# Row variances of a 67 MB array: large loads halved by partitions over two queues, and the columns of a group shared out anew

## The chip, the core and the metric

The kernel runs on one core of a Trainium2 chip. Its engines work side by side: TensorE (not used here), VectorE (DVE), ScalarE (ACT), GpSimd (POOL) and SyncE (SP), which here only issues transfers. ACT can issue transfers too, from its own instruction stream. Data move between HBM and the on-chip memory (SBUF, 128 partitions) by DMA. The metric is the device time of one execution in microseconds (us); lower is better.

## The reference

```python
batch, seq, dim = 32, 512, 1024
x = np.random.randn(batch, seq, dim).astype(np.float32)

mean_sq = np.mean(x**2, axis=-1)
sq_mean = np.mean(x, axis=-1)**2
return (mean_sq - sq_mean).astype(np.float32)
```

For each of the 32 x 512 = 16384 rows of 1024 numbers the output is the mean of the squares minus the square of the mean, which is the variance of the row. 67.1 MB are read and 64 KB are written.

## The kernel before

**Layout.** The 16384 rows are spread over the 128 partitions, 128 rows to each. A row in each of the 128 partitions together is called a column: the kernel has `ncols` = 128 columns of 128 x 1024 numbers, and the result is a tile `mv` whose plane 1 holds one number per partition and column. Rows that lie next to each other in HBM go to the same partition, so n columns of one partition are one piece of n x 4 KB in HBM.

**Stages.** Columns 0 to 103 come in 13 groups of 8 (`GROUP`, `NGROUPS`). A group is one load of 4 MB (`load`, line 45, issued by SP) into a tile `xt` of the pool `xpool`, which has three buffers. So three loads are issued at once, and the load of group g+3 waits until every reader of group g is done. The last 24 columns are the end: loads of 6, 6, 4, 3, 2 and 1 columns, and then two columns in halves of 512 numbers, all into one tile `xt_end` of its own, whose loads wait for no reader.

**Who computes a column.** There are two ways.

- DVE (`dve_halves`, line 111): two `bn_stats` on 512 numbers each, which leave counts, means and sums of squared deviations. In the groups and in the first two end loads these pieces are collected in a tile of statistics and are joined for many columns at once by ten small POOL instructions (`join`, lines 90 to 102). In the later end loads DVE joins them itself with `bn_aggr` (lines 169 and 179).
- ACT (`act_cols`): a `Copy` with a sum over the row, scaled to the negative mean (line 121), and then a `Square` with this mean as its bias and a sum over the row (line 129), which is the variance.

In even groups ACT takes 3 of 8 columns and DVE 5, in odd groups 2 and 6 (`ACT_OF_GROUP`). `END_WHO` names the engine of each end column: 8 go to ACT and 14 to DVE, and the two halved columns go to DVE as well.

**Order.** A scheduler turns this program into one instruction order for each engine and queue and puts in the semaphore waits. In the kernel before, the order on each engine is the order of the program text: 13 group loads, then the ten end loads, then the store of columns 16 to 127 on SP (line 52). The store of columns 0 to 15 stands on ACT between the groups and the end columns. Each engine works through its list strictly in order: an instruction that waits holds everything behind it.

Of the kernel before, what the change touches and what calls it, by code (L numbers as in the profile page):

```python
# [11 lines left out]
def kernel(  # L12
# [8 lines left out]
    nc = tc.nc  # L21
    P = nc.NUM_PARTITIONS
    FP32 = mybir.dt.float32
    ACTF = mybir.ActivationFunctionType
    ALU = mybir.AluOpType

    xf = x.flatten_outer_dims()
    N, D = xf.shape
# [8 lines left out]
    def block_of(c):  # L37
        return next(b for b in BLOCKS if b[0] <= c < b[0] + b[1])

    def load(dst, c0, n, f0=0, f=D):  # L40

        b0, pitch, row0 = block_of(c0)
        assert c0 + n <= b0 + pitch
        ap = [[pitch * D, P], [D, n], [1, f]] if n > 1 else [[pitch * D, P], [1, f]]
        nc.sync.dma_start(  # L45
            out=dst,
            in_=dataclasses.replace(xf, offset=(row0 + c0 - b0) * D + f0, ap=ap),
        )

    def store(engine, block):  # L50
# [6 lines left out]
    GROUP = 8  # L57
    NGROUPS = 13
    END0 = GROUP * NGROUPS
    ACT_OF_GROUP = (3, 2)  # L60

    END_LOADS = [6, 6, 4, 3, 2, 1]
    END_WHO = "AADDDDAADDDDDADDDADADA"
# [2 lines left out]
    xpool = ctx.enter_context(tc.tile_pool(name="xpool", bufs=3))  # L66
    spool = ctx.enter_context(tc.tile_pool(name="spool", bufs=4))
    opool = ctx.enter_context(tc.tile_pool(name="opool", bufs=1))

    mv = opool.tile([P, 2, ncols], FP32)  # L70
    neg_mean = opool.tile([P, ncols], FP32)
    junk = [opool.tile([P, D], mybir.dt.bfloat16, name=f"junk{i}") for i in range(4)]
    xt_end = opool.tile([P, ncols - END0, D], FP32)
    stats_of = {}

    def stats_block(name, groups, each):

        st = opool.tile([P, groups * each, 2, 6], FP32, name=name)
        return st

    def join(st, groups, each, first, step, skip):

        n = groups * each
        part = st.rearrange("p n h (e s) -> p n (h e) s", s=3)
        mean, m2 = part[:, :, :, 1], part[:, :, :, 2]
        two = opool.tile([P, n, 2], FP32, name=f"two{first}")
        mu = opool.tile([P, n, 1], FP32, name=f"mu{first}")
        dev = opool.tile([P, n, 4], FP32, name=f"dev{first}")
        g = nc.gpsimd
        g.tensor_tensor(out=two, in0=mean[:, :, 0:2], in1=mean[:, :, 2:4], op=ALU.add)  # L90
        g.tensor_tensor(out=mu, in0=two[:, :, 0:1], in1=two[:, :, 1:2], op=ALU.add)
        g.tensor_scalar(out=mu, in0=mu, scalar1=0.25, scalar2=None, op0=ALU.mult)  # L92
        g.tensor_tensor(out=dev, in0=mean, in1=mu.to_broadcast([P, n, 4]), op=ALU.subtract)  # L93
        g.tensor_tensor(out=dev, in0=dev, in1=dev, op=ALU.mult)  # L94
        g.tensor_scalar(out=dev, in0=dev, scalar1=D / 4.0, scalar2=None, op0=ALU.mult)  # L95
        g.tensor_tensor(out=dev, in0=dev, in1=m2, op=ALU.add)  # L96
        g.tensor_tensor(out=two, in0=dev[:, :, 0:2], in1=dev[:, :, 2:4], op=ALU.add)  # L97
        g.tensor_tensor(out=mu, in0=two[:, :, 0:1], in1=two[:, :, 1:2], op=ALU.add)
        var = mv[:, 1, first : first + groups * step].rearrange(
            "p (g k) -> p g k", k=step  # L100
        )[:, :, skip : skip + each]
        g.tensor_scalar(  # L102
            out=var,
            in0=mu.rearrange("p (g k) o -> p g (k o)", k=each),
            scalar1=1.0 / D,
            scalar2=None,
            op0=ALU.mult,
        )

    def dve_half(stats, h, xh):  # L110
        nc.vector.bn_stats(out=stats[:, h, :], in_=xh)  # L111

    def dve_halves(stats, xcol):
        dve_half(stats, 0, xcol[:, :H])
        dve_half(stats, 1, xcol[:, H:])

    def act_cols(cols):

        s = D ** -0.5
        for i, (xcol, c) in enumerate(cols):  # L120
            nc.scalar.activation(  # L121
                out=junk[i],
                in_=xcol,
                func=ACTF.Copy,
                scale=-s / D,
                accum_out=neg_mean[:, c : c + 1],
            )
        for i, (xcol, c) in enumerate(cols):
            nc.scalar.activation(  # L129
                out=junk[3],  # L130
                in_=xcol,
                func=ACTF.Square,
                scale=s,
                bias=neg_mean[:, c : c + 1],
                accum_out=mv[:, 1, c : c + 1],
            )

    body = []
    for par in range(2):
        groups = len(range(par, NGROUPS, 2))  # L140
        each = GROUP - ACT_OF_GROUP[par]
        body.append((stats_block(f"stats{par}", groups, each), groups, each))
    for g in range(NGROUPS):
        c0 = g * GROUP
        xt = xpool.tile([P, GROUP, D], FP32, name="xt")
        load(xt, c0, GROUP)
        skip = ACT_OF_GROUP[g % 2]
        act_cols([(xt[:, k, :], c0 + k) for k in range(skip)])
        st, _, each = body[g % 2]
        for k in range(skip, GROUP):  # L150
            dve_halves(st[:, g // 2 * each + k - skip, :, :], xt[:, k, :])
    for par, (st, groups, each) in enumerate(body):
        join(st, groups, each, par * GROUP, 2 * GROUP, ACT_OF_GROUP[par])

    nb, step, skip = BATCH
    each = step - skip
    st_end = stats_block("stats_end", nb, each)
    k = 0
    for b, n in enumerate(END_LOADS):
        load(xt_end[:, k : k + n, :] if n > 1 else xt_end[:, k, :], END0 + k, n)  # L160
        mine = range(k, k + n)
        act_cols([(xt_end[:, j, :], END0 + j) for j in mine if END_WHO[j] == "A"])
        for j in mine:
            if END_WHO[j] == "D" and b < nb:
                dve_halves(st_end[:, b * each + j - k - skip, :, :], xt_end[:, j, :])
            elif END_WHO[j] == "D":
                stats = spool.tile([P, 2, 6], FP32, name="stats")
                dve_halves(stats, xt_end[:, j, :])
                nc.vector.bn_aggr(out=mv[:, :, END0 + j], in_=stats)  # L169
        if b == nb - 1:  # L170
            join(st_end, nb, each, END0, step, skip)
        k += n
    for j in range(k, ncols - END0):
        stats = spool.tile([P, 2, 6], FP32, name="stats")
        for h in range(2):
            xh = xt_end[:, j, h * H : (h + 1) * H]
            load(xh, END0 + j, 1, h * H, H)
            dve_half(stats, h, xh)
        nc.vector.bn_aggr(out=mv[:, :, END0 + j], in_=stats)  # L179
# [33 lines left out]
```

## Time and profile before

| what | value |
|---|---|
| median of 3 runs | 165.49 us (165.44 to 165.92) |
| profiled execution: span from first to last instruction | 163.5 us |
| DVE busy | 106.1 us (65%) |
| ACT busy | 94.9 us (58%) |
| POOL busy | 10.2 us (6%) |
| DMA queue of SP | 67.17 MB, 96.3% of the 16 DMA engines' span |
| mean rate over the span | 411 GB/s |

How to read it: the span runs from the first to the last instruction of one profiled execution. The timed median lies 165.49 - 163.5 = 2.0 us above it, and the prediction carries these 2.0 us along as a constant for what lies around the span. "L121" is line 121 of the kernel. "SPq" and "ACTq" are transfers issued by SP and ACT. In a row of the timeline, the first number is the start and the second the duration, in us; what stands in brackets is how long the engine sat idle and what ended that.

### The profile page before, as it was taken

What the parts mean: (1) busy time and instruction counts of PE and PEld (TensorE: products, weight loads), DVE (VectorE), ACT (ScalarE), POOL (GpSimd) and SP (SyncE); (2) the same over time, 40 slices, a digit from 0 to 9 for tenths busy, and PEclk for the clock granted to TensorE, in tenths of its full rate; (3) what the DMA queues carried; (4) which work ended last, traced back from release to release, by engine and by line L of the source; (5) the groups of instructions that cost most, each with busy time, mean ns of one, the idle gap of its engine ahead of it and who ended that gap; (6) DMA issues with size and microseconds to landing.
All of it is one profiled execution on the core that took longest, in us unless ns stands there. A gap on an engine that the chain in (4) does not pass through costs nothing.

```text
span 163.5 us, 462 instructions
## 1 busy us (share of the span) xinstructions
DVE 106.1 (65%) x182; ACT 94.9 (58%) x165; POOL 10.2 (6%) x34
## 2 busy tenths in 40 slices
DVE  0008559393793917949097682949559396859993
ACT  3008756195733937349390693809755195499892
POOL 0000000000000000000000000000000635302200
DMA  7899898998999999999999999999999999999970
GB/s 257 385 481 417 385 513 385 417 481 385 481 417 385 485 409 393 497 393 425 465 393 473 417 393 505 393 401 489 393 465 425 421 391 475 391 440 409 408 291 14
DMA packets 3602, 67.19 MB, mean 411 GB/s; under 512 B 656, under 2 KB 656, under 8 KB 1296
## 3 DMA queue, kind: packets, MB, share of 16 engines
q1 hardware_dynamic: 3456, 67.17, 96.3%
q10 hardware_dynamic: 144, 0.01, 0.1%
q14 instruction: 2, 0.02, 0.0%
HBM read 67.11 MB, written 0.07 MB: 411 GB/s over the span
## 4 chain that ended last, share of the span: by engine, by line
DMA 79%; DVE 11%; ACT 8%; issue 0%; SPq 0%
DMA xt<-in_x_dram 62%; DMA xt_end<-in_x_dram 17%; DVE stats L111 10%; ACT junk L129 4%; ACT junk L121 4%; DVE mv L179 0%; SPq L45 0%
## 5 line engine op out<-in xcount | busy, mean ns | idle before, releaser
L111 DVE BATCH_NORM_STATS2 stats<-xt 128x6 f32<-128x512 f32 x142 | 85.5, 678 | 50.7 <-DMA xt<-in_x_dram 50.7
L121 ACT ACTIVATE junk<-xt 128x1024 bf16<-128x1024 f32 x33 | 34.5, 1046 | 59.2 <-DMA xt<-in_x_dram 59.2
L129 ACT ACTIVATE junk<-xt,neg_mean 128x1024 bf16<-128x1024 f32 x33 | 37.7, 1142 | 0.6
L111 DVE BATCH_NORM_STATS2 stats_end<-xt_end 128x6 f32<-128x512 f32 x16 | 9.7, 680 | 3.7 <-DMA xt_end<-in_x_dram 3.7
L121 ACT ACTIVATE junk<-xt_end 128x1024 bf16<-128x1024 f32 x8 | 8.4, 1046 | 5.0 <-POOL mv L102 4.2
L111 DVE BATCH_NORM_STATS2 stats<-xt_end 128x6 f32<-128x512 f32 x16 | 10.1, 666 | 0.1
L129 ACT ACTIVATE junk<-xt_end,neg_mean 128x1024 bf16<-128x1024 f32 x8 | 9.2, 1144 | 0.2
L90 POOL TENSOR_TENSOR two<-stats 128x72 f32<-128x72 f32 (+1 forms) x2 | 0.8, 406 | 131.3 <-DVE stats L111 131.3
L129 ACT ACTIVATION_READ_ACCUMULATOR junk<-xt,neg_mean 128x1 f32 x33 | 6.2, 186 | 0.0
L121 ACT ACTIVATION_READ_ACCUMULATOR junk<-xt 128x1 f32 x33 | 6.2, 186 | 0.0
L121 ACT ACT_TABLE_LOAD x1 | 1.3, 1283 | 0.7 <-PEq L197 0.7
L121 ACT ACTIVATION_READ_ACCUMULATOR junk<-xt_end 128x1 f32 x8 | 1.5, 186 | 0.0
L129 ACT ACTIVATION_READ_ACCUMULATOR junk<-xt_end,neg_mean 128x1 f32 x8 | 1.5, 186 | 0.0
L95 POOL TENSOR_SCALAR dev<-dev 128x144 f32<-128x144 f32 (+2 forms) x3 | 1.4, 472 | 0.3
L169 DVE BATCH_NORM_AGGREGATE mv<-stats 128x2 f32<-128x12 f32 x6 | 1.2, 203 | 0.1
L94 POOL TENSOR_TENSOR dev<-dev 128x144 f32<-128x144 f32 (+2 forms) x3 | 1.1, 362 | 0.2
L96 POOL TENSOR_TENSOR dev<-dev,stats 128x144 f32<-128x144 f32 (+1 forms) x2 | 1.1, 528 | 0.2
L93 POOL TENSOR_TENSOR dev<-stats,mu 128x144 f32<-128x144 f32 (+1 forms) x2 | 0.9, 470 | 0.2
L102 POOL TENSOR_SCALAR mv<-mu 128x36 f32<-128x36 f32 (+2 forms) x3 | 0.9, 287 | 0.3
L92 POOL TENSOR_SCALAR mu<-mu 128x36 f32<-128x36 f32 (+2 forms) x3 | 0.9, 284 | 0.3
L97 POOL TENSOR_TENSOR two<-dev 128x72 f32<-128x72 f32 (+2 forms) x3 | 0.8, 276 | 0.2
L90 POOL TENSOR_TENSOR two<-stats_end 128x16 f32<-128x16 f32 x1 | 0.2, 233 | 8.9 <-DVE stats_end L111 8.9
(9 smaller groups left out, 2.7 us busy)
## 6 DMA issues: line engine op xcount, KB each, us to landing
xt<-in_x_dram SPq DMA_DIRECT2D x13, 4096.0 KB, 22.2
xt_end<-in_x_dram SPq DMA_DIRECT2D x2, 3072.0 KB, 32.2
xt_end<-in_x_dram SPq DMA_DIRECT2D x1, 2048.0 KB, 40.0
xt_end<-in_x_dram SPq DMA_DIRECT2D x1, 1536.0 KB, 43.2
xt_end<-in_x_dram SPq DMA_DIRECT2D x1, 1024.0 KB, 45.1
xt_end<-in_x_dram SPq DMA_DIRECT2D x4, 256.0 KB, 15.3
xt_end<-in_x_dram SPq DMA_DIRECT2D x1, 512.0 KB, 36.7
out_dram<-mv SPq DMA_DIRECT2D x1, 56.0 KB, 1.6
```

Source lines behind the costliest of these rows:

```text
L90: g.tensor_tensor(out=two, in0=mean[:, :, 0:2], in1=mean[:, :, 2:4], op=ALU.add)
L92: g.tensor_scalar(out=mu, in0=mu, scalar1=0.25, scalar2=None, op0=ALU.mult)
L93: g.tensor_tensor(out=dev, in0=mean, in1=mu.to_broadcast([P, n, 4]), op=ALU.subtract)
L94: g.tensor_tensor(out=dev, in0=dev, in1=dev, op=ALU.mult)
L95: g.tensor_scalar(out=dev, in0=dev, scalar1=D / 4.0, scalar2=None, op0=ALU.mult)
L96: g.tensor_tensor(out=dev, in0=dev, in1=m2, op=ALU.add)
L97: g.tensor_tensor(out=two, in0=dev[:, :, 0:2], in1=dev[:, :, 2:4], op=ALU.add)
L102: g.tensor_scalar(out=var, in0=mu.rearrange("p (g k) o -> p g (k o)", k=each), scalar1=1.0 / D, scalar2=None, op0=ALU.mult,)
L111: nc.vector.bn_stats(out=stats[:, h, :], in_=xh)
L121: nc.scalar.activation(out=junk[i], in_=xcol, func=ACTF.Copy, scale=-s / D, accum_out=neg_mean[:, c : c + 1],)
L129: nc.scalar.activation(out=junk[3], in_=xcol, func=ACTF.Square, scale=s, bias=neg_mean[:, c : c + 1], accum_out=mv[:, 1, c : c + 1],)
L169: nc.vector.bn_aggr(out=mv[:, :, END0 + j], in_=stats)
```

## The change

- Each of the 13 group loads becomes two of 2 MB: partitions 0 to 63 from SP's queue and partitions 64 to 127 from ACT's queue (`load_group`). Three groups are loaded ahead of the loop, and the load of group g+3 is written behind the work on group g.
- In each group the columns 0 and 1 are treated in a third way: DVE sums both rows with one `tensor_reduce`, ACT squares each with a sum over the row, and three POOL instructions after the loop turn the two sums into the variance for all groups at once. Column 2 is ACT's in the old way, columns 3 to 7 are DVE's in the old way.
- The collected statistics are split by the first seven and the last six groups, and the first join is written behind group 6.
- The end (`END_LOADS`, `END_WHO`) stays as it is in the text.

```diff
-    def load(dst, c0, n, f0=0, f=D):
+    def load(dst, c0, n, f0=0, f=D, p0=0, p=P, engine=nc.sync):
...
-        ap = [[pitch * D, P], [D, n], [1, f]] if n > 1 else [[pitch * D, P], [1, f]]
-        nc.sync.dma_start(
+        ap = [[pitch * D, p], [D, n], [1, f]] if n > 1 else [[pitch * D, p], [1, f]]
+        engine.dma_start(
             out=dst,
-            in_=dataclasses.replace(xf, offset=(row0 + c0 - b0) * D + f0, ap=ap),
+            in_=dataclasses.replace(
+                xf, offset=(row0 + p0 * pitch + c0 - b0) * D + f0, ap=ap
+            ),
         )
...
-    ACT_OF_GROUP = (3, 2)
+    SUMS = 2
+    SKIP = 3
+    AHEAD = 3
...
+    def load_group(g):
+
+        xt = xpool.tile([P, GROUP, D], FP32, name="xt")
+        c0 = g * GROUP
+        load(xt[: P // 2], c0, GROUP, p0=0, p=P // 2)
+        load(xt[P // 2 :], c0, GROUP, p0=P // 2, p=P // 2, engine=nc.scalar)
+        return xt
+
+    each = GROUP - SKIP
+    halves = (NGROUPS + 1) // 2
...
+    total = opool.tile([P, NGROUPS, SUMS], FP32, name="total")
+    meansq = opool.tile([P, NGROUPS, SUMS], FP32, name="meansq")
+    xts = [load_group(g) for g in range(AHEAD)]
     for g in range(NGROUPS):
         c0 = g * GROUP
-        xt = xpool.tile([P, GROUP, D], FP32, name="xt")
-        load(xt, c0, GROUP)
-        skip = ACT_OF_GROUP[g % 2]
-        act_cols([(xt[:, k, :], c0 + k) for k in range(skip)])
-        st, _, each = body[g % 2]
-        for k in range(skip, GROUP):
-            dve_halves(st[:, g // 2 * each + k - skip, :, :], xt[:, k, :])
-    for par, (st, groups, each) in enumerate(body):
-        join(st, groups, each, par * GROUP, 2 * GROUP, ACT_OF_GROUP[par])
+        xt = xts[g]
+        nc.vector.tensor_reduce(
+            out=total[:, g, :], in_=xt[:, :SUMS, :], axis=mybir.AxisListType.X, op=ALU.add
+        )
+        for k in range(SUMS):
+            nc.scalar.activation(
+                out=junk[k],
+                in_=xt[:, k, :],
+                func=ACTF.Square,
+                scale=D ** -0.5,
+                accum_out=meansq[:, g, k : k + 1],
+            )
+        act_cols([(xt[:, k, :], c0 + k) for k in range(SUMS, SKIP)])
+        st = parts[g // halves][0]
+        for k in range(SKIP, GROUP):
+            dve_halves(st[:, g % halves * each + k - SKIP, :, :], xt[:, k, :])
+        if g + AHEAD < NGROUPS:
+            xts.append(load_group(g + AHEAD))
+        if g == halves - 1:
+            join(parts[0][0], halves, each, 0, GROUP, SKIP)
+    join(parts[1][0], NGROUPS - halves, each, halves * GROUP, GROUP, SKIP)
+    sq = opool.tile([P, NGROUPS, SUMS], FP32, name="sq")
+    nc.gpsimd.tensor_tensor(out=sq, in0=total, in1=total, op=ALU.mult)
+    nc.gpsimd.tensor_scalar(out=sq, in0=sq, scalar1=1.0 / (D * D), scalar2=None, op0=ALU.mult)
+    nc.gpsimd.tensor_tensor(
+        out=mv[:, 1, :END0].rearrange("p (g k) -> p g k", k=GROUP)[:, :, :SUMS],
+        in0=meansq,
+        in1=sq,
+        op=ALU.subtract,
+    )
```

The scheduler orders the changed program differently from its text, and this is part of what runs:

- **SP:** the loads of groups 0, 1, 2 (lower halves), the first end load, group 3, the second end load, groups 4 and 5, the third end load, and so on; the last three are the last end half, group 11 and group 12, and then the store.
- **DVE:** the end columns are worked between the groups, in the order in which their loads stand on SP; the last work is group 12.
- **ACT:** three upper-half loads and the table load, then the groups, with the upper-half load of group g+3 among the work of group g+1. All eight end columns stand behind the wait for group 12. Behind this wait come, in this order: a Square of group 12, the Copy of group 11, an end Copy, the Square of group 11, a Square of group 12, an end Copy, the Copy of group 12, the store of columns 0 to 15, the Square of group 12, five pairs of an end Copy and an end Square, one more end Copy, and three end Squares.

More of the change, by code (lines that the diff above doesn't have):

```diff
@@ L73 @@
     xt_end = opool.tile([P, ncols - END0, D], FP32)
-    stats_of = {}
     def stats_block(name, groups, each):
@@ L136, in act_cols @@
             )
[L138 to L142, printed above, removed]
+    def load_group(g):
[5 more added lines that the diff above has]
+    each = GROUP - SKIP
@@ L143 @@
+    halves = (NGROUPS + 1) // 2
+    parts = [(stats_block("stats0", halves, each), halves), (stats_block("stats1", NGROUPS - halves, each), NGROUPS - halves)]
+    total = opool.tile([P, NGROUPS, SUMS], FP32, name="total")
+    meansq = opool.tile([P, NGROUPS, SUMS], FP32, name="meansq")
+    xts = [load_group(g) for g in range(AHEAD)]
     for g in range(NGROUPS):
         c0 = g * GROUP
-        xt = xpool.tile([P, GROUP, D], FP32, name="xt")
-        load(xt, c0, GROUP)
-        skip = ACT_OF_GROUP[g % 2]
```

## The prediction

> **What bounds the kernel now.** I read the page first (busy shares, then the chain that ended last), then the waits, then the engines and DMA by stretches, and last the timeline of the end. The first line below is from the page's busy times, the second from its chain, the next two from the waits (total, times, longest), the next five from the stretches (length; DVE, ACT and POOL busy with their counts; clock; DMA share; GB/s), and the last three from the page's DMA issues (median from issue to landing).
>
> ```profile
> DVE 106.1 (65%) x182; ACT 94.9 (58%) x165; POOL 10.2 (6%) x34
> ...
> DMA 79%; DVE 11%; ACT 8%; issue 0%; SPq 0%
> ...
> ACT junk L121 <- DMA xt<-in_x_dram: 59.2, 13, 10.7
> DVE stats L111 <- DMA xt<-in_x_dram: 50.7, 13, 12.7
> ...
> 20.00:60.00 40.00, 26.50 (x44) 22.80 (x40) 0.00 (x0) 1.00 1.00 431
> 60.00:100.00 40.00, 26.50 (x44) 22.80 (x40) 0.00 (x0) 1.00 1.00 433
> 100.00:140.00 40.00, 29.02 (x49) 22.81 (x40) 6.95 (x18) 1.00 1.00 430
> 158.00:160.00 2.00, 1.97 (x5) 1.97 (x5) 0.00 (x0) 1.00 0.20 74
> 160.00:163.50 3.50, 0.80 (x3) 0.60 (x2) 0.00 (x0) 1.00 0.06 16
> ...
> xt<-in_x_dram SPq DMA_DIRECT2D x13, 4096.0 KB, 22.2
> out_dram<-mv SPq DMA_DIRECT2D x1, 56.0 KB, 1.6
> out_dram<-mv ACTq DMA_DIRECT2D x1, 8.0 KB, 9.0
> ```
>
> No engine is near its limit, and both wait for a load before every group. From 20 to 140 us the DMA engines are busy all the time (share 1.00) at 430 to 433 GB/s. The kernel is the transfer of 67.1 MB plus a start and an end. The last line of the fence matters below: a store of 8 KB on ACT's queue, issued while SP's queue was full, took 9.0 us, the one of 56 KB with nothing beside it 1.6 us. A second queue beside the first therefore does not pass it, it takes turns with its large pieces.
>
> The timeline gives the pace of the loads and the end (start, duration; in brackets idle time and what ended it):
>
> ```profile
> 22.45 7.22 DVE L111 BATCH_NORM_STATS2 stats<-xt 128x6 f32<-128x512 f32 x12 [3.68 <-DMA xt<-in_x_dram]
> ...
> 130.18 6.03 DVE L111 BATCH_NORM_STATS2 stats<-xt 128x6 f32<-128x512 f32 x10 [2.49 <-DMA xt<-in_x_dram]
> ...
> 155.86 1.06 ACT L121 ACTIVATE junk<-xt_end 128x1024 bf16<-128x1024 f32 x1
> 157.04 1.15 ACT L129 ACTIVATE junk<-xt_end,neg_mean 128x1024 bf16<-128x1024 f32 x1
> 158.19 1.04 ACT L121 ACTIVATE junk<-xt_end 128x1024 bf16<-128x1024 f32 x1
> ...
> 159.36 1.23 DVE L111 BATCH_NORM_STATS2 stats<-xt_end 128x6 f32<-128x512 f32 x2
> 160.63 0.21 DVE L179 BATCH_NORM_AGGREGATE mv<-stats 128x2 f32<-128x12 f32 x1
> 160.98 0.35 SPq L52 DMA_DIRECT2D out_dram<-mv  x1
> ```
>
> Group 1 starts at 22.45, group 12 at 130.18: 107.73 / 11 = 9.79 us for 4 MB. Counted back, the stream starts at 22.45 - 2 x 9.79 = 2.9 us. The last two pieces of statistics start at 159.36, right behind the work before them, so the last load landed at about 159.4 (call it T); the end loads took 159.4 - 130.2 = 29.2 us. From the last result (160.84) to the end of the span are 2.7 us of store. So the time is T plus 1.4 of work, 2.7 of store and the 2.0 us between span and median: 165.5.
>
> **The change, part by part.**
>
> *The end.* In the text the end columns come last; in the built order their loads stand among the group loads on SP, so the last thing to land is group 12, and DVE and ACT have work left then. For DVE: one `tensor_reduce` and ten statistics, which took 6.03 us. The `tensor_reduce` is not in the trace; ten statistics at 603 ns each for 512 numbers bound it above (2048 numbers, 2.41 us), and below the same row less 0.11 us of fixed time (an aggregate starts 0.11 to 0.12 us before what follows it): 2048 x (0.603 - 0.11) / 512 + 0.11 = 2.08 us. I take 2.4. Then comes the join, 4.5 us for 35 columns in the trace (136.29 to 140.83). That is T + 13.
>
> ACT is worse. All its eight end columns stand behind its wait for group 12. After T it still has four Squares of groups at 1.15, four Copies at 1.04, an issue of a store at 0.37, five end pairs (Copy to Square 157.04 - 155.86 = 1.18, Square to Copy 158.19 - 157.04 = 1.15, so 2.33), one Copy at 1.18 and three Squares at 1.25 (two in a row in the chain that ended last: 1.25 each): 4.60 + 4.16 + 0.37 + 11.65 + 1.18 + 3.75 = 25.7 us. The Square without a bias is not in the trace; between 1.04 (Copy) and 1.25 it moves this sum by under 0.5. The store on ACT waits for the POOL instruction that subtracts, which needs the last plain Square (T + 5.6) and some 0.3 us more: done before ACT gets there at T + 7.8. The last store on SP waits for ACT's last Square, so POOL's and DVE's T + 13 is covered by ACT. New: time = T + 25.7 + 2.7 + 2.0 = T + 30.4, where it was T + 6.1. This is 24.3 us whatever the loads do, and as ACT idles before each group it has no backlog at T to add.
>
> *DVE and ACT in the groups.* DVE per group 6.03 + 2.4 = 8.4 us instead of 6.03 or 7.22; in all 13 x 8.4 + 21.4 for the end columns (9.7 + 10.1 + 1.2 + 0.4) = 131 us, below the 159 of loads. ACT has 4.6 instead of 4.5 to 6.9. Both lie beside loads at 9.79 us a group or slower: nothing. POOL's three new instructions and the table load, now behind ACT's three issues (1.28 us, beside the first load): nothing.
>
> *Waits and issues.* 26 issues instead of 13, at 0.33 us: beside loads. ACT's last reader of group g now stands behind its wait for group g+1, so the buffer comes free not 7.2 us after landing, but 9.8 + 2.3 = 12.1 us after it. When the next load is issued, group g+2 still has 7.5 us to go, against 2.2 us from the first issue (0.72) to the start of the stream: nothing, with 5 us to spare. Behind ACT's issue, which waits for DVE as well, stand only ACT's own Copies; after an end load of four DVE columns (4.85 us) this wait is up to 1.2 us longer, inside ACT's idle time. SP's end loads need no reader and fill its queue while it waits.
>
> *The halves.* This decides. No row shows a transfer to fewer than 128 partitions. Low end: time goes by bytes, a half takes 4.9 us, and a group 9.79 as now. A gain below that I exclude at the share of 1.00. High end: time goes by the bytes of a partition, a half takes as long as the whole load, and as the two queues take turns by large pieces (the 9.0 us row), a group takes 19.58 us. The nearest row is the whole load: same 32 KB in each partition, same pieces, only fewer partitions. The 9.0 us row also says that the second queue brings no overlap of its own. I take the high end. The end loads keep their 128 partitions; opposite a half, they cost between nothing and their 29.2 us; I take the middle, 14.6. T = 2.9 + 13 x 19.58 + 14.6 = 272.0, and the time 272.0 + 30.4 = 302.4 us; between the bounds for the end loads 288 to 317.
>
> [...]
>
> **The rivals.**
>
> - *The halves run at full speed together.* For it: the DMA share counts 16 engines, and 64 partitions are still enough pieces for all of them. Against it: the nearest row, and the turns of the two queues. Then T = 159.4 and only the end is paid: 189.8 us.
> - *The halves overlap in part.* If engines get out of step, so that some move lower halves while others move upper ones, a group lies between: 14.7 us in the middle. T = 2.9 + 191.1 + 14.6 = 208.6, time 239.0; with the end loads from nothing to 29.2, 224 to 254. For it: a second queue always offers the other half; against it: each queue also runs alone while the other waits for its buffer.
> - *Not slower.* One queue might be what limits the stream, and two lift it. The price of the end must be won back: T = 165.5 - 30.4 = 135.1 and 67.1 MB in 132.2 us, which is 508 GB/s for the whole run. Below that it is slower. The share of 1.00 at 430 GB/s in three stretches of 40 us speaks against it.
> - *The change does not do what it says*, in that DVE gets its relief only on paper (8.4 us a group, more than before): true, but covered by the loads in every case above.
>
> **How the numbers follow.** Halves at the time of whole loads 0.60, since the nearest row and the turns of the queues are both on that side; partial overlap 0.20; full speed 0.19; not slower 0.01. Predicted: 302.4. The range leaves out full speed and takes the partial case from its low end: 224 to 317. The likeliest case alone has 288 to 317. The measurement can tell about 0.3% (0.5 us) from no change; every case but the last is slower by more, and I put 0.005 each on faster and within 0.3%, 0.99 on slower.
>
> **What would show it.** In the profile after: groups of DVE work 19 to 20 us apart (9.8 if I am wrong), a rate of 220 to 260 GB/s for most of the span, and the DMA share still high, since pieces wait in the engines. At the end about 26 us in which ACT alone works on end columns, almost no bytes move, and POOL has long finished; DVE's `tensor_reduce` at 2.1 to 2.4 us. I am wrong in size if the rate holds 430 (then only the end is seen, about 190), and wrong in the sum if ACT does end columns before group 12 lands.

## The result and the profile after

The changed kernel takes 324.01 us (median of six runs, 322.32 to 333.67), against 165.5 before. The ratio is 1.954, with a 95% interval of 1.950 to 1.958. The ratios here leave out slow runs, those more than 1.5% above the fastest of the same kernel: of these six, the ones at 327.83 and 333.67 us. The changed kernel is slower, as forecast, but 7 us beyond the upper end of the range.

From the page after: busy shares, the chain that ended last, and the two queues of the loads (pieces, MB, time of the pieces as a share of the span of all 16 DMA engines; q1 is SP's, q10 ACT's).

```profile
DVE 127.8 (40%) x183; ACT 76.8 (24%) x137; POOL 10.6 (3%) x37
...
DMA 72%; another core or an unknown queue 14%; ACT 11%; issue 2%; ACTq 0%; POOL 0%; POOLq 0%
...
q1 hardware_dynamic: 2624, 39.90, 52.2%
q10 hardware_dynamic: 1184, 27.27, 38.5%
```

The loads still make up most of the chain: no engine is busy even half of the time. (The 14% are steps of the chain whose releaser the trace does not name.) ACT's 11% are mostly the new end. The two queues together fill 90.7% of 322.6 = 292.6 us, all of the time from the start of the stream at about 2.9 us to the last landing at 295.5: the DMA engines hardly ever ran out of pieces. The stretches after (length; DVE, ACT, POOL busy; clock; DMA share; GB/s):

```profile
20.00:60.00 40.00, 16.45 (x22) 8.98 (x15) 0.00 (x0) 1.00 0.98 210
60.00:100.00 40.00, 13.07 (x19) 4.47 (x8) 0.00 (x0) 1.00 1.02 244
100.00:140.00 40.00, 21.90 (x31) 9.56 (x17) 2.36 (x10) 1.00 1.00 259
...
260.00:290.00 30.00, 14.88 (x21) 7.79 (x14) 0.00 (x0) 1.00 1.00 220
290.00:300.00 10.00, 6.89 (x9) 4.47 (x9) 0.52 (x2) 1.00 0.23 60
300.00:310.00 10.00, 3.71 (x7) 9.94 (x19) 3.75 (x11) 1.00 0.01 1
310.00:322.60 12.60, 0.00 (x0) 9.92 (x18) 0.00 (x0) 1.00 0.02 5
```

Up to 290 us the DMA share is 0.98 to 1.02 in these rows, about as before, at 210 to 259 GB/s where it was 430 to 433. So a share near 1.00 says here that pieces are under way, and not that they move at the rate they could. After 295 us almost nothing is moved; from 310 us on ACT works alone. The timeline shows the pace of the groups and the end (start, duration, and in brackets the idle time before):

```profile
25.54 2.29 DVE L158 TENSOR_REDUCE total<-xt 128x2 f32<-128x2048 f32 x1 [25.54 <-DMA xt<-in_x_dram]
...
44.99 2.29 DVE L158 TENSOR_REDUCE total<-xt 128x2 f32<-128x2048 f32 x1 [11.23 <-DMA xt<-in_x_dram]
...
295.48 2.29 DVE L158 TENSOR_REDUCE total<-xt 128x2 f32<-128x2048 f32 x1 [3.11 <-DMA xt<-in_x_dram]
297.68 6.02 DVE L114 BATCH_NORM_STATS2 stats<-xt 128x6 f32<-128x512 f32 x10
...
318.74 1.15 ACT L132 ACTIVATE junk<-xt_end,neg_mean 128x1024 bf16<-128x1024 f32 x1
320.06 0.35 SPq L54 DMA_DIRECT2D out_dram<-mv  x1
```

Groups 0 and 1 start 19.45 us apart. Group 12, the last to land, starts at 295.5 (T); ACT's last Square starts 23.2 us later, and the span ends 27.1 us after T.

### The profile page after: what moved, and what is told of

Its sections match the earlier page's. It is cut to its first block, busy times and chain, and to the rows that moved or that the text cites. A ratio compares the mean times of both kernels' runs of the same rounds, so it can differ in the third digit from the quotient of the medians.

```text
span 322.6 us, 496 instructions
## 1 busy us (share of the span) xinstructions
DVE 127.8 (40%) x183; ACT 76.8 (24%) x137; POOL 10.6 (3%) x37
## 4 chain that ended last, share of the span: by engine, by line
DMA 72%; another core or an unknown queue 14%; ACT 11%; issue 2%; ACTq 0%; POOL 0%; POOLq 0%
DMA xt<-in_x_dram 72%; ACT junk L132 6%; ACT junk L124 3%; ACT junk L162 2%; ACTq L45 0%; ACTq L54 0%; POOL mv L181 0%; ACTq L162 0%; ACTq L241 0%; POOLq L181 0%
## 5 line engine op out<-in xcount | busy, mean ns | idle before, releaser
L162 ACT ACTIVATE junk<-xt 128x1024 bf16<-128x1024 f32 x26 | 27.3, 1048 | 214.4 <-DMA xt<-in_x_dram 214.4
L114 DVE BATCH_NORM_STATS2 stats<-xt 128x6 f32<-128x512 f32 x130 | 78.3, 676 | 0.0
L158 DVE TENSOR_REDUCE total<-xt 128x2 f32<-128x2048 f32 x13 | 29.7, 2286 | 121.0 <-DMA xt<-in_x_dram 121.0
L124 ACT ACTIVATE junk<-xt 128x1024 bf16<-128x1024 f32 x13 | 13.7, 1053 | 8.0 <-DMA xt_end<-in_x_dram 7.7
L132 ACT ACTIVATE junk<-xt,neg_mean 128x1024 bf16<-128x1024 f32 x13 | 14.7, 1133 | 0.0
L162 ACT ACTIVATION_READ_ACCUMULATOR junk<-xt 128x1 f32 x26 | 4.8, 186 | 0.0
L93 POOL TENSOR_TENSOR two<-stats 128x70 f32<-128x70 f32 (+1 forms) x2 | 0.8, 384 | 65.9 <-DVE stats L114 65.9
L132 ACT ACTIVATION_READ_ACCUMULATOR junk<-xt,neg_mean 128x1 f32 x13 | 2.4, 186 | 0.0
L124 ACT ACTIVATION_READ_ACCUMULATOR junk<-xt 128x1 f32 x13 | 2.4, 186 | 0.0
L98 POOL TENSOR_SCALAR dev<-dev 128x32 f32<-128x32 f32 (+2 forms) x3 | 1.4, 454 | 0.3
L97 POOL TENSOR_TENSOR dev<-dev 128x32 f32<-128x32 f32 (+2 forms) x3 | 1.0, 347 | 0.2
L99 POOL TENSOR_TENSOR dev<-dev,stats 128x140 f32<-128x140 f32 (+1 forms) x2 | 1.0, 491 | 0.2
```

The source lines that it names most:

```text
L124: nc.scalar.activation(out=junk[i], in_=xcol, func=ACTF.Copy, scale=-s / D, accum_out=neg_mean[:, c : c + 1],)
L132: nc.scalar.activation(out=junk[3], in_=xcol, func=ACTF.Square, scale=s, bias=neg_mean[:, c : c + 1], accum_out=mv[:, 1, c : c + 1],)
L158: nc.vector.tensor_reduce(out=total[:, g, :], in_=xt[:, :SUMS, :], axis=mybir.AxisListType.X, op=ALU.add)
L162: nc.scalar.activation(out=junk[k], in_=xt[:, k, :], func=ACTF.Square, scale=D ** -0.5, accum_out=meansq[:, g, k : k + 1],)
```

## The experiments

In all tables of stretches below the columns are as above. T is again the time at which the last load lands.

**One queue, both halves by partitions.** The kernel before, with this edit:

```diff
-        load(xt, c0, GROUP)
+        load(xt[: P // 2], c0, GROUP, p0=0, p=P // 2)
+        load(xt[P // 2 :], c0, GROUP, p0=P // 2, p=P // 2)
```

> The kernel before, with only one thing changed: each group load is issued by SP as two loads, partitions 0 to 63 and then 64 to 127. No second queue, same order, same work. Halves theory (64 neighbouring partitions move at half the rate, whoever issues them): groups 19.2 us apart, T = 2.9 + 13 x 19.2 + 29.2 = 281.7, time 281.7 + 6.1 = 288 us. Queue theory (two queues that take turns with large pieces are what is slow): 165.5 us, no change. Theory that the moved order and ACT's waits starve the loads: 165.5 us as well.

Measured: 300.95 us. The timeline and two stretches of this run:

```profile
23.75 6.03 DVE L111 BATCH_NORM_STATS2 stats<-xt 128x6 f32<-128x512 f32 x10 [23.75 <-DMA xt<-in_x_dram]
43.84 7.22 DVE L111 BATCH_NORM_STATS2 stats<-xt 128x6 f32<-128x512 f32 x12 [14.05 <-DMA xt<-in_x_dram]
63.95 6.03 DVE L111 BATCH_NORM_STATS2 stats<-xt 128x6 f32<-128x512 f32 x10 [12.89 <-DMA xt<-in_x_dram]
```

```profile
180.00:220.00 40.00, 13.25 (x22) 11.40 (x20) 0.00 (x0) 1.00 1.00 209
...
270.00:290.00 20.00, 16.46 (x31) 15.20 (x27) 6.18 (x20) 1.00 1.00 422
```

Groups come 20.1 us apart with no second queue and the order of before, and as soon as the loads span 128 partitions again (270 to 290) the rate doubles. The halves are slow by themselves, neither the second queue nor the order makes them so. They are 0.9 us per group slower here than expected (the 19.2 us are an estimate; it agrees with the pieces of the halves in the changed kernel, 64 from each queue to a group at 2.41 and 2.38 us, on 16 engines: 4 x (2.41 + 2.38) = 19.2). Between groups 0 and 1 the pieces of neighbouring partitions lie 64 KB apart in HBM, from group 2 on 448 KB (the columns lie in two blocks, of 16 and of 112 rows to a partition); the pace is the same, 63.95 - 43.84 = 20.1 us, so this distance is not what makes a half slow.

**The lower halves alone.** The kernel before, with `load(xt[: P // 2], c0, GROUP, p=P // 2)` for each group, the work of a group on 64 partitions, and the tiles for the results set to zero at the start by POOL.

> The kernel before, with the upper halves of the group loads left out, and DVE and ACT working on partitions 0 to 63 alone in the groups (the results of the upper 64 partitions are left out; the end is whole). 27 MB less to move. Halves theory: one half alone takes as long as the whole load, groups 9.6 us apart, T = 2.9 + 13 x 9.6 + 29.2 = 157, time 163 us in spite of the missing bytes. Theory that time goes by bytes: a half takes 4.9 us, groups then go at the pace of DVE and ACT, some 7 us, T = 2.9 + 91 + 29.2 = 123, time about 129 us.

Measured: 171.24 us, slower than the kernel before with 27 MB less to move.

```profile
13.85 6.02 DVE L111 BATCH_NORM_STATS2 stats<-xt 64x6 f32<-64x512 f32 x10 [13.85 <-DMA xt<-in_x_dram]
24.04 7.21 DVE L111 BATCH_NORM_STATS2 stats<-xt 64x6 f32<-64x512 f32 x12 [4.17 <-DMA xt<-in_x_dram]
```

```profile
60.00:100.00 40.00, 25.88 (x44) 22.22 (x41) 0.00 (x0) 1.00 1.02 210
100.00:130.00 30.00, 18.66 (x32) 17.65 (x31) 0.00 (x0) 1.00 1.01 208
140.00:155.00 15.00, 11.46 (x20) 10.72 (x19) 3.79 (x10) 1.00 0.99 421
```

A half alone takes 10.2 us, a little more than the whole load took before (9.79). This is the price of a half by itself: the high one of the two bounds in the prediction.

**Halves by columns.** The changed kernel, with this edit:

```diff
-        load(xt[: P // 2], c0, GROUP, p0=0, p=P // 2)
-        load(xt[P // 2 :], c0, GROUP, p0=P // 2, p=P // 2, engine=nc.scalar)
+        load(xt[:, : GROUP // 2, :], c0, GROUP // 2)
+        load(xt[:, GROUP // 2 :, :], c0 + GROUP // 2, GROUP // 2, engine=nc.scalar)
```

> The changed kernel, with each group load halved by columns instead of partitions: columns 0 to 3 of all 128 partitions from SP's queue, columns 4 to 7 from ACT's queue. Same two queues, same number of bytes in each, same instruction orders. Halves theory: full rate, groups 9.8 us apart where no end load comes between, T = 159.4, and only the long end is left: about 190 us. Queue theory: the loads stay slow, 300 us and more.

Measured: 193.53 us.

```profile
20.00:60.00 40.00, 27.34 (x38) 13.41 (x24) 0.00 (x0) 1.00 1.01 430
60.00:100.00 40.00, 34.15 (x50) 13.28 (x24) 3.03 (x13) 1.00 1.00 428
...
160.00:170.00 10.00, 9.06 (x13) 7.47 (x14) 1.18 (x5) 1.00 0.00 0
170.00:180.00 10.00, 0.00 (x0) 8.12 (x15) 3.03 (x9) 1.00 0.01 1
...
171.85 1.15 ACT L132 ACTIVATE junk<-xt,neg_mean 128x1024 bf16<-128x1024 f32 x1 [3.44 <-POOL mv L181]
```

Two queues at once run at the full rate, with the end loads among the groups, and the stream is over at 160 us. What is left of the loss is the long end, 28 us above the 165.6 of the kernel before. Of these, 3.4 are a wait that the changed kernel hardly has: the store on ACT, and with it the Square behind it, waits for the POOL instruction that subtracts, which here comes late, behind the first steps of the join.

**The end loads held back.** The changed kernel, with one instruction more before the second join. POOL writes a number into every column of the tile of the end columns, from a sum that exists only when group 11 is worked on, so the loads into these numbers must wait for it:

```diff
+    nc.gpsimd.tensor_copy(
+        out=xt_end[:, :, 0:1], in_=total[:, NGROUPS - 2, 0:1].unsqueeze(1).to_broadcast([P, ncols - END0, 1])
+    )
```

> The changed kernel, with the end loads (all but half a MB) held back until group 11 is being worked on: POOL copies one number of each column into the tile of the end columns first. So the order is again groups and then end, and the end columns are worked as they land. Halves theory, in which the end loads lost time by running beside halves: T = 2.9 + 13 x 19.2 + 29.2 = 281.7 and the short end, time 288 us. Rival: the halves themselves are slower than 19.2 us per group and the end loads lost nothing: T stays at 295.5, time 302 us.

Measured: 290.17 us.

```profile
254.87 2.29 DVE L158 TENSOR_REDUCE total<-xt 128x2 f32<-128x2048 f32 x1 [10.45 <-DMA xt<-in_x_dram]
```

```profile
140.00:180.00 40.00, 16.47 (x23) 8.98 (x17) 3.79 (x10) 1.00 1.01 224
180.00:220.00 40.00, 18.95 (x24) 11.44 (x21) 0.00 (x0) 1.00 1.01 225
...
260.00:280.00 20.00, 17.77 (x34) 14.61 (x27) 5.91 (x20) 1.00 0.99 419
```

Group 12 starts at 254.9, so a group takes (254.9 - 2.9) / 13 = 19.4 us. The span is 288.4, and 34.2 us shorter than the changed kernel's. DVE works without a break from 274.9 us on, so T does not stand in the timeline. With the 4.1 us of work and store of the kernel before it would be 284.3, where it was 295.5. The last bytes tell much the same, about 282 us here (first fence) and 294 in the changed kernel (second):

```profile
280.00:281.00 1.00, 1.00 (x4) 0.99 (x2) 0.00 (x0) 1.00 0.99 379
282.00:283.00 1.00, 1.00 (x3) 0.97 (x3) 0.00 (x0) 1.00 0.06 25
```

```profile
293.00:294.00 1.00, 0.00 (x0) 0.00 (x0) 0.00 (x0) 1.00 0.23 98
294.00:295.00 1.00, 0.00 (x0) 0.00 (x0) 0.00 (x0) 1.00 0.00 0
```

So of the 34.2 us, 22 to 23 are the end, and 11 to 12 come from end loads that no longer run beside halves. Which of the two loses time when they run side by side stands in the trace, piece by piece. The pieces of the halves (32 KB) took 2.41 us on SP's queue and 2.38 us on ACT's in the changed kernel, and 2.40 and 2.39 us here. The pieces of the end loads, added up and shared out over the 16 engines, took 42.7 us there and 31.5 us here; in the kernel before it was 29.8 us. The loss sits in the end loads.

**Halves by even and odd partitions.** The changed kernel, with `load(xt[0 : P : 2], ..., pstep=2)` on SP and `load(xt[1 : P : 2], ..., pstep=2, engine=nc.scalar)` on ACT; `pstep` multiplies the partition step of the source.

> The changed kernel, with each group load halved into even partitions (SP) and odd partitions (ACT) instead of lower and upper ones. Bytes, queues, pieces and orders stay. [...] In-step theory (a half is slow because the 16 engines work through their four pieces in step, and at each moment two of them are at the same place; each engine has four neighbours of the list, so even partitions do not help): 300 to 325 us. [...]

Measured: 189.28 us.

```profile
20.00:60.00 40.00, 28.81 (x41) 13.40 (x24) 0.00 (x0) 1.00 0.99 426
60.00:100.00 40.00, 31.82 (x48) 12.22 (x22) 2.37 (x10) 1.00 1.00 431
100.00:140.00 40.00, 35.34 (x55) 14.60 (x27) 3.78 (x10) 1.00 1.02 434
```

Same queues, same bytes, same pieces of 32 KB, 64 partitions per load as well: full rate. A piece of a half takes 1.23 us on SP's queue and 1.22 on ACT's, where it took 2.41 and 2.38, and the pieces of the end loads take 29.8 us, as in the kernel before. What makes a half slow is that its partitions are neighbours; why they are slow, the runs do not show. The in-step theory, as I had laid the pieces to the engines, falls. With the partitions, the rows that a load reads from HBM change too, and no run varies one without the other. Against HBM as the cause speaks that the whole loads read the same rows at full rate, and that the halves are equally slow at two distances (20.1 us a group in the run with one queue).

**The new sharing of the columns alone.** The changed kernel with `load(xt, c0, GROUP)`, one load per group on SP.

> The changed kernel with one load per group on SP again, 128 partitions: the change's new sharing of the columns alone. Its built order is groups and then end. Theory that DVE's and ACT's new work is covered: 165.5 us, the same within 0.5. Rival: DVE at 8.3 us a group (2.29 + 6.02) against a landing every 9.8 us is late at the end, where DVE works 16 columns in 29 us: up to 2 us slower.

Measured: 165.72 us against 165.62, ratio 1.0009 (0.9998 to 1.002). The stretches show DVE busier than before and the loads untouched:

```profile
20.00:60.00 40.00, 33.90 (x46) 17.87 (x32) 0.00 (x0) 1.00 1.00 432
60.00:100.00 40.00, 32.89 (x44) 17.88 (x32) 3.79 (x10) 1.00 1.00 432
100.00:140.00 40.00, 34.34 (x47) 20.23 (x37) 1.87 (x7) 1.00 1.00 430
...
99.76 10.04 SPq L45 DMA_DIRECT2D xt<-in_x_dram  x2
109.85 36.10 SPq L45 DMA_DIRECT2D xt_end<-in_x_dram  x10
```

The sums on DVE, the plain Squares on ACT and the three POOL instructions cost nothing. It also shows where the moved order comes from: with one load per group on SP, the built order is groups and then end again (the last two lines, from SP's timeline). Whether two loads per group or the issue from ACT moves it, no run tells apart.

**Halves by columns, end loads held back.**

> Halves by columns over the two queues, as in the run before that had them, and the end loads held back until group 11 is being worked on. Theory that two queues at 128 partitions are neither better nor worse than one: the end is short again, T about 160, time 165.5 to 168 us. Rival, two queues fill gaps that one leaves: the stream ends 1 us earlier at best (share 0.94 in the first 20 us), 164.5 us. Rival, the held loads come late: a gap of some us before the end, 168 to 172 us.

Measured: 167.59, 167.62, 170.5 and 170.6 us in four runs; the profiled one is that of 167.59 (span 165.8), near the upper end of the first expectation. Two queues at 128 partitions bring nothing over one.

**One load ahead, to put the engines out of step.** The changed kernel with the end loads held back and, ahead of all other loads, `load(xt_end[:8, :16, :], END0, 16, p0=0, p=8)`.

> The changed kernel with the end loads held back (290 us), and one more load ahead of all others on SP: 64 KB into each of 8 partitions of the tile of the end columns, which is loaded again later. 8 partitions keep only 8 of the 16 engines busy, so one half of the engines starts on the halves up to 2.4 us, one slow piece, behind the other. In-step theory: the engines that collided are now at different halves at the same moment, groups come 9.8 to 16 us apart while both queues are full, time 185 to 260 us. Theory that a half is slow in itself, however its engines stand to each other: groups 18.8 us apart as before, 290 to 295 us; the same if the extra load is cut in two pieces, which take a turn each.

Measured: 306.05 us.

```profile
31.89 2.29 DVE L159 TENSOR_REDUCE total<-xt 128x2 f32<-128x2048 f32 x1 [31.89 <-DMA xt<-in_x_dram]
51.29 2.29 DVE L159 TENSOR_REDUCE total<-xt 128x2 f32<-128x2048 f32 x1 [11.18 <-DMA xt<-in_x_dram]
```

The first group lands 6.4 us later than without the extra load, and the groups then come 19.4 us apart. By the expectation this speaks for halves that are slow in themselves, but the extra load was itself slow (118 GB/s in the first 10 us, against 206 in the changed kernel), and the profile does not show how far apart it left the engines. The packets fit the 8 engines of the expectation: 8 more under 512 B with the extra load (872 against 864), where each of the 13 additional group loads of the change brought 16 (864 against 656). I count it as inconclusive.

**The even partitions alone.** The twin of the lower halves: the kernel before, with three fixed tiles set to zero at the start, and `load(xt[0 : P : 2], c0, GROUP, p=P // 2, pstep=2)`.

> The twin of the run with lower halves alone: the kernel before, with only the even partitions of the group loads loaded (the odd partitions are set to zero once at the start, in three fixed tiles, and their results are left out; DVE and ACT work on all 128 partitions). [...] Theory that any 64 partitions are slow when they are alone, and that even and odd halves only helped each other: groups 10 us apart, 170 to 185 us.

Measured: 132.69 us, far below the 170 to 185 us of the theory that any 64 partitions are slow when they are alone. The next fence has two stretches of this run, the two after it the median time of a group's load from issue to landing, here and with the lower halves alone:

```profile
20.00:60.00 40.00, 40.00 (x69) 35.68 (x65) 0.00 (x0) 1.00 0.81 310
60.00:100.00 40.00, 40.00 (x68) 34.90 (x63) 0.00 (x0) 1.00 0.86 334
```

```profile
xt<-in_x_dram SPq DMA_DIRECT2D x13, 2048.0 KB, 7.6
```

```profile
xt<-in_x_dram SPq DMA_DIRECT2D x13, 2048.0 KB, 23.5
```

DVE never stops, the loads wait for it (share 0.81 and 0.86), and still more bytes come per microsecond than with the lower halves at a share of 1.0. So 64 partitions are not slow as such, even alone.

**Even and odd partitions, end loads held back.** Both causes taken away, the rest of the change kept.

> Halves by even and odd partitions over the two queues, and the end loads held back until group 11 is being worked on, so that both causes of the loss are gone and the rest of the change stays. Theory that these two are all of it: 165.5 to 168 us, the upper part where the held loads leave a gap, as with halves by columns (167.6). If something of the change were still unnamed: above 170 us. If two queues were of use once the halves are spread: below 165 us.

Measured: 167.91 us, ratio 1.0141 (1.0124 to 1.0158) to the kernel before. Nothing large of the change is unnamed. The 2.4 us that remain were not followed up; DVE ends its work at 163.2 us in this run, 2.4 us later than in the kernel before (160.8).

## Why the prediction was right and wrong

The verdict (slower) and the end that ACT works off alone were right. The price of a half was right in size, but for a reason that the runs refute. The time left the range because of one term, the end loads.

| step of the sum | predicted | measured |
|---|---|---|
| start of the stream | 2.9 | 2.9 (taken over) |
| 13 groups | 13 x 19.58 = 254.5 | 13 x 19.4 = 252.2 (with the end loads held back) |
| end loads | 0 to 29.2, taken 14.6 | 295.5 - 2.9 - 252.2 = 40.4 (what is left) |
| from T to the time | 30.4 | 324.4 - 295.5 = 28.9 |
| sum | 302.4 | 324.4 (the profiled execution; the median is 324.0) |

- **The end loads are the step that failed.** The prediction said: "opposite a half, they cost between nothing and their 29.2 us; I take the middle, 14.6". I had no reason to leave out a loss: that two transfers side by side could cost more than one after the other did not enter the bounds. The end loads cost 40.4 us as what is left of the sum; added up piece by piece it is 42.7 us of the 16 engines' time, against 29.8 in the kernel before. The runs show that the slow halves beside them are the cause. With even and odd halves the same end loads stand among the groups in much the same places and take 29.8 us; with halves by columns, too, the whole stream is over by 160 us. With slow halves but the end loads behind them it is 31.5 us, and T is 11 to 12 us earlier. The halves themselves take no longer beside the end loads. How a slow piece holds up the others was not shown.
- **The halves.** Right in size, within 1%, but by luck in the reason. I took the price from the bytes per partition, because the whole load was the nearest row. Even and odd halves have the same 32 KB per partition and the same 64 partitions to a load, and run at 426 to 434 GB/s, so time does not go by the bytes of a partition; it is the choice of the partitions that counts, and the prediction did not ask which ones they are. Nor did it need the second queue taking turns (the store's 9.0 us): one queue is slow too (20.1 us a group, against 19.4 with two).
- **The end.** 28.9 instead of 30.4. Instruction by instruction the count was right; ACT's last Square started 23.2 us after T. The wait for group 12 did hold what stands behind it: the first end load had landed by 87.6 us, when DVE began on its columns, and ACT, which has two of its six columns, started its first end Copy at 297.6. In the end pairs a Square followed its Copy after 1.03 to 1.17 us, where I took 1.18.
- **DVE, ACT, POOL, waits and issues at nothing:** right; the sharing alone is 165.72 us, and with even and odd halves the stream ran at the full rate in spite of the waits and issues. The `tensor_reduce` took 2.29 us, between the bounds 2.08 and 2.41.
- **The rivals.** Full speed (189.8) is what the halves gave once their partitions were not neighbours: 189.28. The partial overlap did not appear: 19.4 us a group, not 14.7. The "not slower" case was out of reach.

## What to carry to other kernels

Where DMA is the bound, keep each load across all 128 partitions (430 to 433 GB/s here), or split it by columns (425 to 430) or by even and odd partitions (426 to 434), which here gained nothing but lost nothing in rate; a split into lower and upper partitions halved it, on one queue (205 to 210) as on two (213 to 225 with the end loads held back). The DMA share in the profile stayed near 1.00 (0.98 to 1.03 from 20 to 290 us) and hid this, so look at GB/s. Look at the built instruction order and not at the text: splitting the loads moved the end columns behind the last group on ACT, and that alone cost 22 to 23 us. When a term can hide or collide, bound it on both sides: a transfer beside a slow one can cost more than it does alone (42.7 us here, against 29.8).

## What was not expected

- 64 even partitions load at 310 to 334 GB/s with the loads waiting for DVE, 64 neighbouring ones at 210 GB/s with nothing in their way. The number of partitions does not tell the rate; which ones they are does.
- Loads to all 128 partitions cost 40.4 us beside slow halves instead of 29.2, although the halves beside them are no slower for it (2.41 and 2.38 us a piece, against 2.40 and 2.39 without them).
- Halves of neighbours are a little slower from one queue (20.1 us a group) than from two (19.4), so the second queue did bring something, 4% where 100% would have been needed.
